# The scan stage of a hybrid linear-attention layer: squares of finished rows put behind the copies of the largest level, attention heads taken by PSUM bank, state and output products of one direction together

## The chip, the core and the metric

The kernel runs on one core of a Trainium2 chip. The time is the device time of one execution in microseconds. TensorE (PE) has two clock levels in the profile, 1.2 and 2.4 GHz; the column "PEclk" of a view gives the granted clock as a share of the higher one.

## What is computed

One layer over 2048 latent tokens (16 chunks of 128 rows here) after a prefix of 256 context tokens (two chunks). Two bidirectional linear-attention mixers run on the same normalized input: GLA (a gate for each key dimension, 4 heads of 64 keys and 128 values) and Gated DeltaNet (delta rule, 4 heads of 128). Each latent scan starts from the last context state of its direction. In the scan stage, per chunk and direction:

```
# GLA
att = einsum('bhtd,bhsd,bhtsd->bhts', q, k, exp(b_t - b_s))      # causal, decay for each key dimension
o   = einsum('bhtd,bhde->bhte', q * exp(b), s) + att @ v
s   = s * exp(b_last) + einsum('bhsd,bhse->bhde', k * exp(b_last - b), v)
# Gated DeltaNet
v_new = u - w @ s
o     = (q * exp(g)) @ s + aqk @ v_new
s     = s * exp(g_last) + (k * exp(g_last - g))^T @ v_new
# both: the two directions are added, then
y = rmsnorm(o_f + rev(o_b), onorm) * silu(gate)
```

After the scan stage both y go through their output weights, are merged by gates and projected; a residual and a last RMSNorm follow.

## The kernel before, in words

The program runs in three stretches: projections and preparation (to about 1366 us), the scan stage (`phase_mix`, 1366 to 1812), the output products (from 1812, where PE is full again). The change lies in the scan stage alone.

The scan stage has a context step and 16 latent steps. Step `si` takes one chunk from the front (direction 0, "f") and one from the back (direction 1, "b"). In step s the GLA attention of the new pair is built (`gla_step`), and the outputs of the pair loaded a step earlier are made: GDN by `gdn_scan`, one generator for each direction, GLA by `gla_state` and `gla_out`. From the middle on every chunk has been met by both directions, so each step finishes four rows of heads: two of GDN (tile `oi`) and two of GLA (tile `og`). `finish` then takes the squares of the finished row (four instructions on ACT, L1409, with an accumulator read each), a logarithm and an exponential as root (L1410, L1411, ACT), the product (L1412, POOL), four transposes (L1416, PE) and the product with the gate (L1417, DVE); until then (the first half) the outputs go to DRAM.

The order on each engine comes from three things. The generators are woven: `weave` gives each its turn in a fixed proportion, and a `yield` ends a turn. A list scheduler then orders all instructions by program order as priority, by waits, and by the slots of the tile pools; an engine runs its instructions in the order that results. Last, `behind` ties one instruction after another in that order, without a semaphore.

The pieces that the change and the prediction speak of:

- `gdn_scan`: L1055 (w @ s), L1066 (q @ s), L1077 (v_new, read by DVE L1079 into `vn`), then the state product L1087 (read by DVE L1091 into `Sb`) and the output product L1097 (read by DVE L1098 into `oi`). Each is 4 matmuls in the program, 8 in the trace, for a direction. All put their result into a PSUM tile `pz`, of which there are three in rotation.
- `gla_group`: decay sums (L1125, PE, from the gate g that ACT L132 splits into halves after its load), exponentials (L1213, L1216, ACT), products with q (L1222, DVE, `ql`) and k (L1223, POOL, `E`).
- `gla_lev`: level products (L1264, PE), in two groups a step: 32 instructions in the program for levels 64, 32, 16, 8 (64 in the trace), then 16 for levels 4 and 2. The level 64 is copied by ACT (L1272) into `at`, the others by DVE into `own` (L1275). The second group waits for its PSUM slots to be read.
- `gla_ones` and `gla_near`: level 1; DVE L1238 and POOL L1239 make `qk`, PE L1246 multiplies it, ACT L1236 its exponential, L1252 copies `own` into `at`.
- `gla_out`: the products of attention and v (L1346) go into two PSUM tiles, heads 0 and 2 into the first, 1 and 3 into the second; L1354 adds the products with the state; ACT (L1362) or DVE (L1364) reads them into `og`.

```
        for h in range(4):
            nc.tensor.matmul(po[h % 2][:, 0, h // 2], f["at"][:, h], f["v"][:, h * P:(h + 1) * P],
                             start=h < 2, stop=False, skip_group_check=True)
```

Of the kernel before, what the change touches and what calls it, by code (L numbers as in the profile page):

```python
# [16 lines left out]
AF = mybir.ActivationFunctionType  # L17
# [80 lines left out]
class Build:  # L98
# [945 lines left out]
    def gdn_scan(self, r, need_o, end=False):  # L1044
        nc, wk = self.nc, self.wk
        d, c = r["d"], r["c"]
        S = self.Sb[d]
        B4 = [P, 4, P]
        col = lambda t, h: t[:, c, 4 * d + h:4 * d + h + 1]
        if S is None:  # L1050
            rhs = r["v"]
        else:
            ps = self.heads(self.pv())
            for h in range(4):
                nc.tensor.matmul(ps[:, h], r["kT"][:, h, :], S[:, h], start=True, stop=True)  # L1055
            rhs = wk.tile(B4, F32, name="rhs")
            for h in range(4):
                nc.vector.scalar_tensor_tensor(rhs[:, h], ps[:, h], col(self.negeg, h), r["v"][:, h],
                                               op0=ALU.mult, op1=ALU.add)
            yield  # L1060
        if need_o:
            l = c - NCTX
            prev = r["prev"]
            po = self.heads(self.pv())
            for h in range(4):
                mm = nc.tensor.matmul(po[:, h], r["qT"][:, h, :], S[:, h], start=True, stop=True)  # L1066
            self.fin_rest(2, mm)
            oi = prev if prev is not None else self.op.tile(B4, F32, name="oi", bufs=4)
            for h in range(4):
                if prev is None:  # L1070
                    nc.scalar.mul(oi[:, h], po[:, h], col(self.eg, h))
                else:
                    nc.vector.scalar_tensor_tensor(oi[:, h], po[:, h], col(self.eg, h), prev[:, h], op0=ALU.mult, op1=ALU.add)
            yield
        ps = self.heads(self.pv())
        for h in range(4):
            nc.tensor.matmul(ps[:, h], r["ub"][:, h], rhs[:, h], start=True, stop=True)  # L1077
        vn = wk.tile(B4, F32, name="vn")
        nc.vector.tensor_tensor(vn, ps, self.bc(self.beta, c, d), op=ALU.mult)  # L1079
        yield  # L1080
        if not end:
            S2 = self.st.tile(B4, F32, name=f"Sb{d}")
            if S is not None:
                nc.gpsimd.tensor_tensor(S2, S, self.bc(self.egl, c, d), op=ALU.mult)
            ps = self.heads(self.pv())
            for h in range(4):
                nc.tensor.matmul(ps[:, h], r["kt"][:, h], vn[:, h], start=True, stop=True)  # L1087
            if S is None:
                nc.vector.tensor_copy(S2, ps)
            else:  # L1090
                nc.vector.tensor_tensor(S2, S2, ps, op=ALU.add)  # L1091
            self.Sb[d] = S2
            yield
        if need_o:
            po = self.heads(self.pv())
            for h in range(4):
                nc.tensor.matmul(po[:, h], r["at"][:, h], vn[:, h], start=True, stop=True)  # L1097
            nc.vector.tensor_tensor(oi, po, oi, op=ALU.add)  # L1098
            yield
            yield from self.put_o(1, l, oi)  # L1100
# [153 lines left out]
    def gla_lev(self, levs, behind=None):  # L1254
        nc, got = self.nc, []
        for r, ks, ql, m in levs:
            ps = self.slot()
            for ct in range(2):
                for x in range(2):
                    y = x if m < 64 else 1 - x  # L1260
                    keys, qs = slice(64 * x, 64 * x + 64), slice(64 * y, 64 * y + 64)
                    for hp in range(2):
                        rows = slice(64 * hp, 64 * hp + 64)
                        mm = nc.tensor.matmul(ps[keys, hp, ct], ks[ct][rows, keys], ql[rows, ct, qs], start=True, stop=True)  # L1264
                        self.behind(mm, behind)
                        self.last_lev = mm
            got.append((r, ps, m))
        for r, ps, m in got:
            if m == 64:
                for x in range(2):  # L1270
                    rows, cols = slice(64 * x, 64 * x + 64), slice(64 - 64 * x, 128 - 64 * x)
                    nc.scalar.copy(self.byhalf(r["at"])[rows, :, :, cols], ps[rows])  # L1272
            else:
                i = LEVELS.index(m) - 1
                nc.vector.copy_predicated(self.byhalf(r["own"]),  # L1275
                                          self.am[:, i].unsqueeze(1).unsqueeze(1).broadcast_to([P, 2, 2, 64]), ps)
# [64 lines left out]
    def gla_out(self, pair, S):  # L1341
        nc = self.nc
        f = pair[0]
        po = [self.pv().rearrange("p (d c t) -> p d c t", d=2, c=2) for _ in range(2)]
        for h in range(4):
            nc.tensor.matmul(po[h % 2][:, 0, h // 2], f["at"][:, h], f["v"][:, h * P:(h + 1) * P],  # L1346
                             start=h < 2, stop=False, skip_group_check=True)
        for d, r in enumerate(pair):
            for ct in range(2):
                for x in range(2):  # L1350
                    half = slice(64 * x, 64 * x + 64)
                    for hp in range(2):
                        rows = slice(64 * hp, 64 * hp + 64)
                        mm = nc.tensor.matmul(po[hp][half, d, ct], r["qe"][rows, ct, half], S[d][rows, ct], start=False,  # L1354
                                              stop=d == 1 and ct == 1, skip_group_check=True)

        def done():
            o = self.og = f["prev"] if f["prev"] is not None else self.op.tile([P, 2, 4, P], F32, name="og")
            v = lambda t, hp: t.rearrange("p d (c h) t -> p h d c t", h=2)[:, hp]
            for hp in range(2):  # L1360
                if f["prev"] is None:
                    nc.scalar.copy(v(o, hp), po[hp])  # L1362
                else:
                    nc.vector.tensor_tensor(v(o, hp), v(f["prev"], hp), po[hp], op=ALU.add)  # L1364
        return mm, done
# [34 lines left out]
    def finish(self, mi, l, src):  # L1400
        nc, wk = self.nc, self.wk
        if "o" in self.dbg:
            nc.sync.dma_start(self.dbg["o"][mi, l], self.flat(src))
        y = wk.tile([P, 4, P], F32, name="fg", bufs=4)
        nc.sync.dma_start(y, self.d_gb[l, :, 4 * mi:4 * mi + 4, :])
        sq = wk.tile([P, P], BF16, name="fsq", bufs=1)
        ss = wk.tile([P, 4], F32, name="fss", bufs=4)
        for h in range(4):
            nc.scalar.activation(sq, src[:, h], AF.Square, accum_out=ss[:, h:h + 1])  # L1409
        nc.scalar.activation(ss, ss, AF.Ln, bias=self.eps, scale=1.0 / 128)  # L1410
        nc.scalar.activation(ss, ss, AF.Exp, scale=-0.5)  # L1411
        nc.gpsimd.tensor_tensor(src, src, ss.unsqueeze(2).broadcast_to([P, 4, P]), op=ALU.mult)  # L1412
        mm = yield
        pt = self.pe()
        for h in range(4):
            self.behind(nc.tensor.transpose(pt[:, h * P:(h + 1) * P], src[:, h], self.ident), mm)  # L1416
        nc.vector.scalar_tensor_tensor(self.flat(y), pt, self.pc[:, 64 + mi:65 + mi], self.flat(y),  # L1417
                                       op0=ALU.mult, op1=ALU.mult)
        nc.sync.dma_start(self.d_y[l, :, mi * 4:mi * 4 + 4, :], y)
        yield  # L1420
# [18 lines left out]
    def phase_mix(self):  # L1439
        nc = self.nc  # L1440
# [26 lines left out]
        self.gq = self.pool("gq", 2, ctx=gctx)  # L1467
        self.ppe = self.pool("ppe", 3, PSUM, ctx=ctx)
        self.lv = self.pool("ppg", 1, PSUM, ctx=gctx).tile([P, 2, 4, 2, 64], F32, name="lv")
        self.nslot, self.last_lev = 0, None  # L1470
        self.seen, self.fin = [{}, {}], []
        self.Sa, self.Sb = [None, None], [None, None]
        order = [(2 + s, NCH - 1 - s) for s in range(NLAT)]
# [425 lines left out]
```

## Time and profile before

| | |
|---|---|
| median of 3 runs | 2144.94 us (2143.9 to 2147.0) |
| profiled execution | 2138.93 us, span of its instructions 2136.9 us |
| mean granted clock | 0.987 |
| busy, share of the span | PE 96%, DVE 60%, ACT 43%, POOL 38% |
| scan stage, 1366 to 1812 us | PE 393.2 of 446 us busy, granted clock 0.96 |
| before it and after it | PE 1334.6 of 1366 us and 314.1 of 324.9 us, clock 1.00 and 0.99 |

A step of the scan is measured from one first L1264 to the next; these begin at 1385.66 (first latent step), 1415.85, 1439.38, 1464.12, 1486.05, 1510.13, 1531.99, 1554.13, 1578.21, 1599.78, 1625.91, 1653.97, 1679.61, 1706.00, 1734.43 and 1761.10 us. Finished rows begin with the step from 1599.78.

How to read the views: a group of equal instructions is written as engine, line, operation, output<-inputs, shapes, count. "[0.38 <-DVE oi L1098]" is the time in which the engine stood still before the group, and the instruction whose end released it. Busy times of the stretches are sums within the stretch; DMA share is that of the core's 16 DMA engines.

### The profile page before, as it was taken

How to read it: one execution, taken by the hardware profiler on the slowest of the kernel's cores; microseconds unless marked ns; L12 is line 12 of the kernel's file. 1: busy time of each engine (PE TensorE's matmuls, PEld its weight loads, DVE VectorE, ACT ScalarE, POOL GpSimd, SP SyncE). 2: the span in 40 equal slices, each digit the busy share in tenths (PEclk: the TensorE clock that was granted, in tenths of full speed). 3: DMA queues.
4: the chain of work that ended last, by engine and by line, in shares of the span. 5: the costliest groups of instructions: out<-in, count | busy, mean ns of one | idle time of the engine just before them, and what ended most of it. 6: DMA issues, size and time to landing. Idle time of an engine off the chain costs nothing.

```text
span 2136.9 us, 40356 instructions
## 1 busy us (share of the span) xinstructions
PE 2041.9 (96%) x15208; PEld 1674.4 (78%) x15208; DVE 1283.2 (60%) x2229; ACT 914.5 (43%) x2208; POOL 816.7 (38%) x746
## 2 busy tenths in 40 slices
PE   6999999999999999999999999899988888999998
PEld 2688888888888888777777777688888876787786
DVE  2713555556667653555555655466567776576776
ACT  3645245555543223444344444345545656002332
POOL 2410122222221104566666665256556656002211
PEclk9999999999999999999999999999999999999999
DMA  8323122222222224443344443688888877898543
GB/s 285 111 86 119 48 58 76 63 62 65 73 63 72 72 72 133 149 143 129 122 146 141 159 144 110 202 306 284 296 291 297 296 250 233 286 317 300 181 147 111
DMA packets 272862, 346.96 MB, mean 162 GB/s; under 512 B 25000, under 2 KB 176796, under 8 KB 272668
## 3 DMA queue, kind: packets, MB, share of 16 engines
q1 hardware_dynamic: 272668, 344.39, 48.8%
q8 instruction: 120, 1.97, 0.4%
q14 instruction: 74, 0.61, 0.1%
HBM read 218.73 MB, written 125.57 MB: 161 GB/s over the span
## 4 chain that ended last, share of the span: by engine, by line
PE 72%; DMA 7%; issue 7%; DVE 6%; ACT 5%; POOL 3%; SPq 1%; DVEq 0%; POOLq 0%; ACTq 0%
PE pz L371 46%; PE pm L1605 3%; PE pz L1605 2%; DMA g<-dg 2%; PE pe L943 1%; PE pe L1125 1%; PE pl L1002 1%; PE pl L995 1%; PE pz L1087 1%; DMA ga<-dgate 1%; PE pl L1003 1%; DVE ql L1222 1%; ACT E L1216 1%; PE pp L1823 1%; PE pz L1066 1%
## 5 line engine op out<-in xcount | busy, mean ns | idle before, releaser
L371 PE MATMUL pz<-hi,wh 128*128 128x512 f32 (+1 forms) x1560 | 621.2, 399 | 1.1 <-DVE hi L134 1.1
L371 PE MATMUL pz<-lo,wh 128*128 128x512 f32 (+1 forms) x1560 | 600.1, 385 | 1.8 <-POOL lo L135 1.8
L371 PE MATMUL pz<-hi,wl 128*128 128x512 f32 (+1 forms) x1520 | 588.1, 387 | 0.0
L371 PEld LDWEIGHTS pz<-lo,wh 128*128 128x128 f32 x1560 | 294.6, 189 | 51.2 <-POOL lo L135 3.7
L371 PEld LDWEIGHTS pz<-hi,wh 128*128 128x128 f32 x1560 | 294.1, 189 | 47.1 <-DVE hi L134 1.7
L371 PEld LDWEIGHTS pz<-hi,wl 128*128 128x128 f32 x1520 | 285.9, 188 | 53.7 <-issue 0.4
L135 POOL TENSOR_TENSOR wl<-w,wh 128x1024 fp32r<-128x1024 f32 x44 | 109.6, 2491 | 437.5 <-ACT wh L132 314.2
L575 DVE SCALAR_TENSOR_TENSOR acc<-zpad,cw,acc 128x1024 f32<-128x1024 f32 x192 | 269.5, 1403 | 6.6
L880 DVE CAST_PREDICATED U<-kit,pl 128x256 f16<-128x256 int32 x216 | 91.3, 432 | 138.7 <-PE pl L1003 135.0
L996 ACT CAST ppb<-pl 128x256 f16<-128x256 f32 x216 | 73.8, 374 | 169.9 <-PE pl L995 163.2
L1605 PE MATMUL pm<-y,wb 128*128 128x512 f32 x480 | 118.5, 399 | 5.2 <-DVE ga L1608 2.9
L1223 POOL TENSOR_TENSOR E<-E,ak 128x256 f32<-128x256 f32 x96 | 79.4, 847 | 111.5 <-ACT E L1216 67.0
L135 DVE TENSOR_TENSOR sql<-sq,sqh 128x512 fp32r<-128x512 f32 (+1 forms) x36 | 28.0, 804 | 142.7 <-ACT sqh L132 142.5
L1605 PEld LDWEIGHTS pm<-y,wb 128*128 128x128 f32 x480 | 90.9, 191 | 26.9 <-DVE y L135 2.6
L630 POOL TENSOR_TENSOR acc<-acc,sq 128x512 f32<-128x512 f32 x32 | 50.6, 1590 | 138.7 <-ACT sq L629 90.9
L560 ACT COPY zpad<-pz 128x512 f32<-128x512 f32 x48 | 28.2, 588 | 137.5 <-PE pz L371 137.5
L1125 PE MATMUL pe<-wt,gh 128*128 128x256 f32 x264 | 77.0, 320 | 8.8 <-ACT E L1216 4.9
L880 DVE CAST_PREDICATED Tm<-kit,pl 128x256 f16<-128x256 int32 x180 | 76.4, 425 | 0.0
L1002 PEld LDWEIGHTS <-Tm 128*128 128x128 f16 x864 | 55.1, 98 | 26.5 <-issue 22.0
L132 ACT CAST wh<-w 128x1024 fp32r<-128x1024 f32 x44 | 46.2, 1049 | 68.6 <-PE pz L371 56.0
L1216 ACT ACTIVATE E<-pe 128x128 f32<-128x128 f32 x320 | 64.5, 306 | 18.7 <-PE pe L1125 18.1
L1222 DVE TENSOR_TENSOR ql<-E,q 128x256 f32<-128x256 f32 x96 | 64.1, 694 | 13.6 <-ACT E L1213 11.7
(326 smaller groups left out, 4265.3 us busy)
## 6 DMA issues: line engine op xcount, KB each, us to landing
gd<-dgd SPq DMA_DIRECT2D x32, 768.0 KB, 7.8
w<-in_w_in SPq DMA_DIRECT2D x44, 512.0 KB, 3.5
dgate<-ob SPq DMA_DIRECT2D x128, 128.0 KB, 1.8
qk<-dqkv SPq DMA_DIRECT2D x32, 512.0 KB, 5.9
ga<-dgate SPq DMA_DIRECT2D x64, 256.0 KB, 4.7
x<-in_x SPq DMA_DIRECT2D x28, 512.0 KB, 5.0
dqkv<-acc SPq DMA_DIRECT2D x192, 64.0 KB, 1.6
dgd<-tm SPq DMA_DIRECT2D x36, 256.0 KB, 2.5
```

What stands on the lines that cost most here:

```text
L135: getattr(nc, lo).tensor_tensor(dst_lo, src, dst_hi.bitcast(F32), op=ALU.subtract)
L371: nc.tensor.matmul(ps[:, 0:n], a[:, kk, :], b[:, kk, :], start=(k == 0), stop=(k == last - 1))
L575: nc.vector.scalar_tensor_tensor(acc, src, wcol, acc, op0=ALU.mult, op1=ALU.add)
L630: nc.gpsimd.tensor_tensor(v, v, r, op=ALU.mult)
L880: self.nc.vector.copy_predicated(out, mv, data)
L996: nc.scalar.copy(ppl, pc.rearrange("p h (j i) -> p h j i", i=m))
L1002: nc.tensor.matmul(pu[:, h], Tm[:, h], ppl[:, h], start=True, stop=True)
L1125: self.nc.tensor.matmul(out, g[:, i, ct * P:(ct + 1) * P], self.wt[:, d, cols[0]:cols[1]], start=(j == 0), stop=(j == 1))
L1216: nc.scalar.activation(E[:, ct, li, x].rearrange("p (j e i) -> p e j i", e=2, i=m), s[:, x * P:(x + 1) * P].rearrange("p (e j i) -> p e j ...
L1222: nc.vector.tensor_tensor(ql[:, li], E[:, :, li, 0], q, op=ALU.mult)
L1223: nc.gpsimd.tensor_tensor(E[:, :, li, 1], E[:, :, li, 1], k, op=ALU.mult)
L1605: nc.tensor.matmul(ps, self.wab[j // 2][wi][:, 4 * i + k, (j % 2) * P:(j % 2) * P + P], yy[:, k, :], start=(n == 0), stop=(n == 11))
```

## The change

No instruction is added or removed. A `yield` between the state and the output product of a direction goes, so the two are issued in one turn; `gla_out` takes the heads in the order 0, 2, 1, 3; the ACT copies of level 64 are remembered as `self.far`, and the squares in `finish` are tied behind the last of them.

```diff
@@ gdn_scan
                 nc.vector.tensor_tensor(S2, S2, ps, op=ALU.add)
             self.Sb[d] = S2
-            yield
         if need_o:
@@ gla_lev
-                    nc.scalar.copy(self.byhalf(r["at"])[rows, :, :, cols], ps[rows])
+                    self.far = nc.scalar.copy(self.byhalf(r["at"])[rows, :, :, cols], ps[rows])
@@ gla_out
-        for h in range(4):
+        for h in (0, 2, 1, 3):
@@ finish
-            nc.scalar.activation(sq, src[:, h], AF.Square, accum_out=ss[:, h:h + 1])
+            self.behind(nc.scalar.activation(sq, src[:, h], AF.Square, accum_out=ss[:, h:h + 1]), self.far)
@@ phase_mix
-        self.nslot, self.last_lev = 0, None
+        self.nslot, self.last_lev, self.far = 0, None, None
```

Below, lines after 1093 are one lower in the changed kernel (L1097 is L1096 there, L1272 is L1271, L1409 is L1408). PE at the end of a first-half step, before (`vn`, `gd`, `av` are the inputs named above; gh and gl the halves of the gate):

```order
L1087 MATMUL pz<-vn,gd 128x128 x8
L1125 MATMUL pe<-wt,gh_16745 128x2x128
L1125 MATMUL pe<-wt,gl_16746 128x2x128
L1125 MATMUL pe<-wt,gh_16745 128x2x2x64
L1125 MATMUL pe<-wt,gl_16746 128x2x2x64
L1143 MATMUL pe<-kf,E_16776 128x128 x2
L1097 MATMUL pz<-vn,gd 128x128 x8
L1346 MATMUL pz<-av,at 128x128 x4
L1354 MATMUL pz<-Sa_16461,q_16381 64x128 x8
```

and the same place in the changed kernel:

```order
L1087 MATMUL pz<-vn,gd 128x128 x4
L1096 MATMUL pz<-vn,gd 128x128 x4
L1087 MATMUL pz<-vn,gd 128x128 x4
L1096 MATMUL pz<-vn,gd 128x128 x4
L1124 MATMUL pe<-wt,gh_16745 128x2x128
L1124 MATMUL pe<-wt,gl_16746 128x2x128
L1124 MATMUL pe<-wt,gh_16745 128x2x2x64
L1124 MATMUL pe<-wt,gl_16746 128x2x2x64
L1142 MATMUL pe<-kf,E_16776 128x128 x2
L1345 MATMUL pz<-av,at 128x128 x4
L1353 MATMUL pz<-Sa_16461,q_16381 64x128 x8
```

The output product of direction 0 moved ahead of the state product of direction 1, and four L1125 moved behind both outputs. DVE at the same place, before:

```order
L1079 TENSOR_TENSOR vn<-pz,beta 128x512
L1091 TENSOR_TENSOR Sb_17224<-Sb_17224,pz 128x512
L1091 TENSOR_TENSOR Sb_17232<-Sb_17232,pz 128x512
L1222 TENSOR_TENSOR ql<-E,q_17061 128x256 x2
L1098 TENSOR_TENSOR oi<-pz,oi 128x512 x2
```

and changed:

```order
L1079 TENSOR_TENSOR vn<-pz,beta 128x512
L1091 TENSOR_TENSOR Sb_17224<-Sb_17224,pz 128x512
L1097 TENSOR_TENSOR oi<-pz,oi 128x512
L1091 TENSOR_TENSOR Sb_17238<-Sb_17238,pz 128x512
L1097 TENSOR_TENSOR oi<-pz,oi 128x512
L1221 TENSOR_TENSOR ql<-E,q_17061 128x256 x2
```

Each `oi` moved right behind its `Sb`, ahead of the two `ql`. ACT in a second-half step, from the copies of level 64 on, before:

```order
L1409 ACTIVATE fsq,fss<-og 128x128 x4
L1272 COPY at<-lv 64x2x2x64 x2
L1216 ACTIVATE E<-pe 128x2x16x4 x2
L1216 ACTIVATE E<-pe 128x2x32x2 x2
L1145 COPY akt<-pe 128x256
L1236 ACTIVATE E_18799<-pe 128x128 x2
L1410 ACTIVATE fss<-fss,cb 128x4
L1409 ACTIVATE fsq,fss<-oi 128x128
L1411 ACTIVATE fss<-fss 128x4
L1409 ACTIVATE fsq,fss<-oi 128x128 x3
```

and changed:

```order
L1271 COPY at<-lv 64x2x2x64 x2
L1215 ACTIVATE E<-pe 128x2x16x4 x2
L1215 ACTIVATE E<-pe 128x2x32x2 x2
L1144 COPY akt<-pe 128x256
L1235 ACTIVATE E_18799<-pe 128x128 x2
L1408 ACTIVATE fsq,fss<-oi 128x128 x4
L1409 ACTIVATE fss<-fss,cb 128x4
L1408 ACTIVATE fsq,fss<-oi 128x128
L1410 ACTIVATE fss<-fss 128x4
L1408 ACTIVATE fsq,fss<-oi 128x128 x2
```

The four squares of the first og moved from ahead of the copies to behind all squares of oi. The products of `finish` follow on POOL (og's L1412 behind those of oi) and PE (L1416: oi, oi, og, og in place of og, oi, oi, og, with all eight matmuls of L1077 ahead of the last).

## Rows read from the trace of the kernel before

**Rows 1.** The page: busy time, share of the span and number of matmuls of PE; the chain that ended last, share of the span by engine.

```profile
PE 2041.9 (96%) x15208; PEld 1674.4 (78%) x15208; DVE 1283.2 (60%) x2229; ACT 914.5 (43%) x2208; POOL 816.7 (38%) x746
...
PE 72%; DMA 7%; issue 7%; DVE 6%; ACT 5%; POOL 3%; SPq 1%; DVEq 0%; POOLq 0%; ACTq 0%
```

**Rows 2.** The table by stretch. Columns: from:to us, length, then busy us (and instructions) of PE, PE's weight loads, DVE, ACT, POOL, then granted clock, DMA share, GB/s. The stretches are eight steps, six steps, and two single steps.

```profile
1415.85:1599.78 183.93, 167.92 (x2280) 153.64 (x2276) 118.61 (x267) 97.93 (x364) 107.25 (x130) 0.99 0.82 289
1599.78:1761.10 161.32, 140.92 (x1766) 131.10 (x1762) 121.07 (x276) 94.75 (x458) 101.05 (x116) 0.95 0.84 285
1415.85:1439.38 23.53, 22.51 (x317) 19.63 (x313) 14.69 (x33) 12.28 (x46) 13.47 (x16) 1.00 0.86 319
1653.97:1679.61 25.64, 22.13 (x299) 20.31 (x295) 20.05 (x46) 15.77 (x76) 17.36 (x20) 1.00 0.90 295
```

**Rows 3.** What PE waited for from 1368 to 1600 us (the first half and the context step). Columns: us in total, times, longest.

```profile
PE pz L1346 <- DVE oi L1098: 5.9, 8, 1.9
PE pz L1087 <- DVE vn L1079: 5.0, 9, 1.3
PE lv L1264 <- POOL E L1223: 3.4, 10, 0.4
```

**Rows 4.** The timeline of PE in the first half: one step's end, and two L1087 of which the first direction waits. Columns: start, length in us, engine, line, operation, and the wait before it.

```profile
1408.87 2.05 PE L1087 MATMUL pz<-vn,gd 128*128 128x128 f32 x16 [0.61 <-DVE vn L1079]
...
1456.70 1.05 PE L1087 MATMUL pz<-vn,gd 128*128 128x128 f32 x8
1458.08 1.16 PE L1087 MATMUL pz<-vn,gd 128*128 128x128 f32 x8 [0.33 <-DVE vn L1079]
...
1459.78 1.95 PE L1097 MATMUL pz<-vn,gd 128*128 128x128 f32 x16
1461.56 0.39 PE L1346 MATMUL pz<-av,at 128*128 128x128 f32 x2
1462.33 0.94 PE L1346 MATMUL pz<-av,at 128*128 128x128 f32 x6 [0.38 <-DVE oi L1098]
...
1593.98 2.05 PE L1087 MATMUL pz<-vn,gd 128*128 128x128 f32 x16 [1.34 <-DVE vn L1079]
```

**Rows 5.** The timeline of all engines around PE's longest wait of the first half, columns as in rows 4.

```profile
1502.91 1.17 ACT L132 CAST gh<-g 128x512 fp32r<-128x512 f32 x2 [2.07 <-DMA g<-dg]
...
1504.29 2.05 DVE L1222 TENSOR_TENSOR ql<-E,q 128x256 f32<-128x256 f32 x2 [1.10 <-ACT E L1216]
...
1506.99 1.45 PE L1346 MATMUL pz<-av,at 128*128 128x128 f32 x6 [1.90 <-DVE oi L1098]
```

**Rows 6.** The table by stretch, columns as in rows 2: three stretches of low granted clock.

```profile
1507.40:1510.90 3.50, 3.50 (x74) 3.28 (x76) 0.14 (x1) 0.49 (x2) 1.88 (x3) 0.53 0.49 181
1722.40:1725.70 3.30, 3.30 (x17) 3.30 (x16) 1.79 (x5) 0.72 (x3) 0.15 (x1) 0.50 0.68 224
1633.80:1640.20 6.40, 6.40 (x37) 6.05 (x38) 3.93 (x13) 4.57 (x22) 4.99 (x6) 0.50 0.62 182
```

**Rows 7.** What PE waited for from 1600 to 1812 us (the second half), columns as in rows 3.

```profile
PE lv L1264 <- DVE own L1275: 6.8, 6, 1.5
PE pe L1246 <- POOL qk L1239: 6.1, 6, 1.5
PE pe L1416 <- POOL og L1412: 6.0, 4, 2.5
```

**Rows 8.** The timeline of all engines in the step from 1706.00 us, columns as in rows 4.

```profile
1706.00 1.11 PE L1264 MATMUL lv<-ql,E 64*64 64x64 f32 x64
...
1706.96 0.31 ACT L1409 ACTIVATE fsq<-og 128x128 bf16<-128x128 f32 x1 [5.86 <-DVE og L1364]
...
1708.05 0.31 ACT L1409 ACTIVATE fsq<-og 128x128 bf16<-128x128 f32 x1
...
1708.48 0.31 ACT L1409 ACTIVATE fsq<-og 128x128 bf16<-128x128 f32 x1
...
1708.79 0.73 ACT L1272 COPY at<-lv 64x256 f32<-64x256 f32 x2
...
1710.44 0.51 ACT L1236 ACTIVATE E<-pe 128x128 f32<-128x128 f32 x2
...
1711.69 0.69 PE L1264 MATMUL lv<-ql,E 64*64 64x64 f32 x32 [0.79 <-DVE own L1275]
1711.73 1.08 POOL L1412 TENSOR_TENSOR og<-og,fss 128x512 f32<-128x512 f32 x1
...
1713.82 0.61 PE L1246 MATMUL pe<-bones,qk 128*128 128x2 f32 x4 [1.01 <-POOL qk L1239]
...
1717.09 0.40 ACT L1252 COPY at<-own 64x256 f32<-64x256 f32 x1
...
1718.90 0.62 ACT L132 CAST gh<-g 128x512 fp32r<-128x512 f32 x1 [1.08 <-DMA g<-dg]
...
1721.92 0.81 PE L1416 MATMUL pe<-kf,og 128*128 128x128 f32 x4 [2.28 <-POOL og L1412]
...
1730.73 1.95 PE L1097 MATMUL pz<-vn,gd 128*128 128x128 f32 x16
1732.52 1.06 PE L1346 MATMUL pz<-av,at 128*128 128x128 f32 x8
1733.50 1.10 PE L1354 MATMUL pz<-Sa,q 64*64 64x128 f32 x32
```

## The prediction

> **What bounds the kernel now.** I read the page first [rows 1]: TensorE (PE) is busy for 2041.9 us, 96% of the span, and the chain that ended last runs through it for 72%, so only what stops PE, or lowers its clock, can move the time. Then the table by stretch [rows 2]: the scan stage is where PE is not full. Its first eight latent steps after the first (from 1415.85 us; no row is finished yet) take 183.93 us with 167.92 busy, 23.0 us a step; the six from 1599.78 (rows are finished, their squares run on ACT) take 161.32 with 140.92 busy, 26.9 a step. Granted clock 0.99 and 0.95: the second part loses clock as well as time. Then PE's waits in each half [rows 3, 7], and the timelines of single steps for what stands ahead of each wait [rows 4, 5, 8]. The reader is to see that the first half's waits are short, on DVE, and at two places, and the second half's sit behind one long ACT queue.
>
> **First half: state and output products of one direction together.** No instruction is added or removed; all of the change is order. Now PE runs L1087 for both directions, then L1097 for both, then L1346. Two waits follow from this.
>
> (a) The second direction's L1087 waits for its vn, which DVE makes last: 0.33 us in the step shown [rows 4]. Of the 5.0 us in 9 such waits [rows 3] two are the first direction's (0.61 and 1.34, [rows 4]) and stay, since nothing is put ahead of them. The other seven are 3.05 us. In the new order the first direction's L1097 (eight matmuls; the sixteen of both directions take 1.78) stands between: 0.9 us of cover against waits of 0.3 to 0.6. I take all 3.05 as removed.
>
> (b) L1346 stops after two of its matmuls, for a PSUM buffer that DVE frees by oi L1098: 5.9 us, 8 times, longest 1.9 [rows 3], 0.38 in the step shown [rows 4]. DVE does Sb, Sb, two ql, and only then the two oi. The buffers rotate by three, so L1346's second buffer is the one that held the first direction's output. In the new order this output starts right behind the first direction's L1087, at 1457.6 instead of 1459.78 in the step shown, its oi runs right behind its Sb, ahead of the ql, and the buffers asked for are those of the first oi and the second Sb. I take 5.9 as removed. The head order (0, 2, 1, 3) moves the use of the second buffer two matmuls later, 0.22 us; once the wait is gone that is worth nothing. What changing buffers at every matmul costs by itself is bounded by eight L1346 in 0.98 us against 0.90 for eight L1097 [rows 8]: at most 0.1 a step, 1.5 over all steps; I take 0, since L1346 also ends in matmuls of another shape.
>
> (c) The longest of these, 1.90 us, was ACT's cast waiting 2.07 us for the DMA of g, then ql, then oi [rows 5]. Behind it the clock stood at 0.53 for 3.5 us [rows 6]: the lower level, 1.2 GHz, after PE had stood still. At half speed 3.5 us do the work of 1.86, so 1.64 us go with it.
>
> What it may cost: the four L1125 that stood between L1087 and L1097 now come behind both outputs, so exp (ACT), ql (DVE) and E (POOL) for the next L1264 start later. From the step shown I place the last E 0.3 us ahead of its use: bounds 0 and, from L1264's wait on E that is there already (3.4 us in 10, [rows 3]), another 0.4 a step, 3.2 in all. I take 1.0, nearer the end where it is hidden. Sum of the first half: -3.05 - 5.9 - 1.64 + 1.0 = **-9.6 us**.
>
> **Loads.** The first half moves 289 GB/s x 183.93 us = 53.2 MB; at the most a step of the trace shows, 319 GB/s [rows 2], that is 167 us. The shortened half needs about 175 (one of the eight L1346 waits lies ahead of it), so transfers allow it, with 5% to spare. The Trainium skill (Perfetto Trace Analysis, Roofline) puts the ceiling of one core's 16 DMA engines at about 435 GB/s; by that the estimate is 122 us, and no step here comes near that rate. Both leave the sum as it is; the thin margin of the measured rate is the reason for a rival.
>
> **Second half: squares behind the copies.** Now ACT holds four squares of og ahead of the at copies. They wait for DVE's og (5.86 us idle before the first) and run one every 0.43 us, so the copies start 2.8 us into the step [rows 8]. DVE's own waits for the copies, PE's second L1264 for own (0.79), and POOL, with og's L1412 (1.08) ahead of qk's L1239, holds PE's L1246 (1.01) [rows 8]. In all: own 6.8 us, qk 6.1, and L1416 on og 6.0 [rows 7], 18.9 us over the six steps and the last one, 2.7 a step.
>
> After: the copies start when the first L1264 ends, at about +1.1 us; L1236 ends near +3.9 where it now ends at 1710.95, +4.95. The waits on own and qk (12.9 us) go. But all sixteen squares stand behind L1236 now, not twelve. From L1236's end to the last square now takes 6.5 us (to 1717.49, the end of the L1252 behind it [rows 8]); four squares more are 1.74, a cast of gh and the roots about 0.9, and the cast waits for its DMA, 1.08 in this step: the last og is normalized by L1412 (1.08) and reaches PE at 3.9 + 6.5 + 1.74 + 0.9 + 1.08 + 1.08 = +15.2 us; without the DMA wait +14.1. PE came to its last og L1416 at 1719.64, +13.6, with 0.79 and 1.01 of waits that go and with four L1077 (0.9) that now come before it: +12.7. So PE waits 1.4 to 2.5 us at its two og transposes, where 2.7 a step go now. The work behind them is the same. Bounds: 1.3 a step gained, or, with twice the DMA wait, 3.6 waited and 0.9 lost; I take **0**, by the row with the DMA wait in it. That POOL now runs og's L1412 behind those of oi costs nothing more: it is made when ACT's root comes.
>
> Clock: 0.95 over 161.32 us is 16 us at 1.2 GHz, 8 us lost. The 2.28 us wait was followed by 0.50 over 3.3 us [rows 6, 8]; the step at 1653.97, with four short waits, kept 1.00 [rows 2]. The new waits are few and long, so I leave the 8 us as it is. The Trainium skill (TensorE: Matmul & The Clock Gate, A second HAM failure mode) says the reverse: frequent micro-idles between groups of matmuls make the clock fall and rise. By that, merging four waits into two would give clock back; the trace bears it out less than the other reading, and what it would give is the third rival.
>
> The context step ahead and the last step are reordered too; I see nothing on the path there: 0, bounds +-2 us.
>
> **Sum**: -9.6 + 0 + 0 = -9.6 us on a profiled execution of 2138.93. That one is 6.0 us under the median of the runs, 2144.94; against the median the forecast is 2135.3. About 0.2% (4.3 us) is what a measurement can tell from no change.
>
> **Rivals.**
> 1. *The squares' tail decides (slower).* Every second-half step waits 3.6 us at og, and the clock falls behind it for 6.4 us, as it did once [rows 6]: 3.2 us lost a step. Over 6.5 steps (the last counted half): 6.5 x 0.9 + 6.5 x 3.2 - 8 = +18.7, less 9.6: 2154. It decides from +2.1 us a step. For: the ACT chain is longer than PE's way to the transposes. Against: the chain starts 1.05 us earlier.
> 2. *The first half gives it back.* The g loads are late already (2.07, [rows 5]); what PE gains it loses at E or ql. Half of 9.6 stays, and the second half costs 2: 2142.
> 3. *The clock comes back.* PE's waits in the second half merge and the 8 us go: 2127.5. For: 2.7 us of waits at three places become 1.4 at one. Against: the 2.28 us wait of [rows 8].
> 4. *The order does not change as said*, so nothing happens. The printed order of PE, ACT and DVE excludes that; I give it no chance.
>
> **Chances.** Forecast 0.54 (2131 to 2140, by the bounds 0 to 3.2 and +-2); rival 3 0.18; rival 2 0.18; rival 1 0.10. Faster 0.72, same 0.18, slower 0.10. The range goes from a little beyond rival 3, 2126, to between rivals 2 and 1, 2146.
>
> **What would show it.** In the changed profile: L1346 without a wait on oi, and the second L1087 without one on vn; eight first-half steps in about 175 us at clock 1.00; L1264's wait on E below 0.8. In the second half: no wait on own, a shorter one on qk, L1416 on og at 10 to 18 us in all, steps near 26.9, copies at +1.1 and the last square near +12 to +14. The forecast is wrong if L1264 waits over 1 us on E or ql in the first half, if second-half steps differ from 26.9 by over 1 us, or if stages outside the scan move.

## The result, and the profile after

| | before | changed |
|---|---|---|
| first comparison, median | 2144.42 us (6 runs) | 2126.41 us (2123.3 to 2130.07, 6 runs) |
| ratio, 95% interval | | 0.9922 [0.9904, 0.9941] |
| second comparison | 2140.76 us (17 runs) | 2128.32 us (6 runs), 0.9934 [0.9919, 0.9949] |
| profiled executions | 2138.93, span 2136.9 | 2126.90, span 2125.1 |

The change is faster by 0.7 to 0.8%; 2135.3 us with a range of 2126.0 to 2146.0 had been forecast, so the first median lies 0.4 us inside the range. The two profiled executions differ by 12.0 us, the first medians by 18.0. The table by stretch of the changed kernel (columns as in rows 2; eight first-half steps, six finishing steps, and a piece of the first finishing step), from one L1353 to the next, answers to [rows 2]:

```profile
1416.37:1589.27 172.90, 165.02 (x2274) 151.81 (x2273) 121.51 (x268) 97.23 (x363) 107.16 (x130) 1.00 0.86 302
1589.27:1748.35 159.08, 138.37 (x1753) 128.66 (x1752) 122.34 (x276) 95.00 (x455) 102.86 (x117) 0.96 0.87 296
1603.00:1611.00 8.00, 5.44 (x28) 5.44 (x29) 2.65 (x7) 5.42 (x28) 5.16 (x6) 0.57 0.71 224
```

The first half goes from 183.93 to 172.90 us at clock 1.00, the six finishing steps (those from which finished rows are made) from 161.32 to 159.08 at clock 0.96. The context step ends 1.4 us later, and what follows the six steps takes 376.8 us for 376.7. PE's waits in the first half (us in total, times, longest; [rows 3] before):

```profile
PE lv L1263 <- POOL E L1222: 5.5, 14, 0.8
...
PE pz L1087 <- DVE vn L1079: 1.2, 2, 0.7
```

L1346 (now L1345) waits no more, and of the waits on vn the two of the first direction are left. The wait on E has grown, from 3.4 us in 10. The same place as in [rows 4], PE's timeline in the changed kernel:

```profile
1456.05 1.05 PE L1087 MATMUL pz<-vn,gd 128*128 128x128 f32 x8
1456.94 1.06 PE L1096 MATMUL pz<-vn,gd 128*128 128x128 f32 x8
1458.03 1.16 PE L1087 MATMUL pz<-vn,gd 128*128 128x128 f32 x8
1459.02 1.06 PE L1096 MATMUL pz<-vn,gd 128*128 128x128 f32 x8
...
1460.61 1.06 PE L1345 MATMUL pz<-av,at 128*128 128x128 f32 x8
1461.60 1.10 PE L1353 MATMUL pz<-Sa,q 64*64 64x128 f32 x32
1462.52 1.11 PE L1263 MATMUL lv<-ql,E 64*64 64x64 f32 x64
```

The four products of the two directions run one behind the other, and L1345 runs its eight matmuls in one piece: no group has a wait in brackets. PE's waits in the second half ([rows 7] before):

```profile
PE pe L1415 <- POOL oi L1411: 10.6, 3, 4.4
PE pe L1415 <- POOL og L1411: 7.7, 6, 2.4
PE lv L1263 <- POOL E L1222: 3.9, 11, 0.6
...
PE pe L1245 <- POOL qk L1238: 0.8, 1, 0.8
```

None is on own any more and 0.8 us is left on qk, but 18.3 us are at the transposes (L1415), 10.6 of them on oi, in three waits. The timeline of all engines in the first finishing step shows what stands ahead of one of these:

```profile
1591.37 0.75 ACT L1271 COPY at<-lv 64x256 f32<-64x256 f32 x2 [0.43 <-PE lv L1263]
...
1593.68 0.56 ACT L1235 ACTIVATE E<-pe 128x128 f32<-128x128 f32 x2
...
1596.44 0.31 ACT L1408 ACTIVATE fsq<-oi 128x128 bf16<-128x128 f32 x1
...
1601.88 0.62 ACT L132 CAST gh<-g 128x512 fp32r<-128x512 f32 x1 [5.03 <-DMA g<-dg]
...
1602.40 0.30 ACT L1408 ACTIVATE fsq<-oi 128x128 bf16<-128x128 f32 x1
...
1604.47 1.03 POOL L1411 TENSOR_TENSOR oi<-oi,fss 128x512 f32<-128x512 f32 x1
...
1605.56 1.12 PE L1415 MATMUL pe<-kf,oi 128*128 128x128 f32 x4 [4.39 <-POOL oi L1411]
```

The copies start 1.2 us after the L1263 at 1590.19, as intended. But between two squares of oi stands the cast gh, which waits 5.03 us for its load. The squares behind it are late, then POOL's product, then PE, which waits 4.39 us, and the granted clock is 0.57 from 1603 to 1611 us (last row of the table above).

### The profile page after: what moved, and what is told of

The parts are those of the page before. It is cut to its first block, busy times and chain, and to the rows that moved or that the text cites. A ratio compares the mean times of both kernels' runs of the same rounds, so it can differ in the third digit from the quotient of the medians.

```text
span 2125.1 us, 40362 instructions
## 1 busy us (share of the span) xinstructions
PE 2037.5 (96%) x15208; PEld 1670.0 (79%) x15208; DVE 1282.5 (60%) x2229; ACT 914.1 (43%) x2208; POOL 818.2 (38%) x746
## 4 chain that ended last, share of the span: by engine, by line
PE 71%; DMA 9%; issue 6%; POOL 5%; DVE 4%; ACT 4%; SPq 1%; DVEq 0%; POOLq 0%; ACTq 0%
PE pz L371 46%; PE pm L1604 3%; DMA g<-dg 2%; PE pz L1604 2%; PE pe L943 1%; PE pl L1002 1%; PE pl L995 1%; PE pl L1003 1%; POOL E L1222 1%; DMA dm<-ga 1%; PE pe L1124 1%; PE pp L1822 1%; PE pq L620 1%; PE pz L1087 1%; PE pz L1077 1%
## 5 line engine op out<-in xcount | busy, mean ns | idle before, releaser
L630 POOL TENSOR_TENSOR acc<-acc,sq 128x512 f32<-128x512 f32 x32 | 51.3, 1611 | 137.8 <-ACT sq L629 89.9
L1124 PE MATMUL pe<-wt,gh 128*128 128x256 f32 x264 | 74.7, 313 | 4.5 <-ACT E L1133 2.7
```

What stands on the lines that cost most here:

```text
L630: nc.gpsimd.tensor_tensor(v, v, r, op=ALU.mult)
L1124: self.nc.tensor.matmul(out, g[:, i, ct * P:(ct + 1) * P], self.wt[:, d, cols[0]:cols[1]], start=(j == 0), stop=(j == 1))
```

## Experiments

Lengths of the six finishing steps, from one L1354 (L1353) to the next, us; the ratio is to the runs of before in the same comparison, on one chip, with its 95% interval. Beside the first comparison there are three, each on its own chip: e0, e1, e2 and e4; e5, e7, e8 and e9; e10, e11, e12 and a0.

```
kernel                          first half  finishing steps 1 to 6                    ratio
before                          183.93      26.12 28.06 25.64 26.40 28.42 26.68
before again (a0_before)        180.66      26.37 26.13 27.56 27.70 28.37 25.12       0.9994 [0.9981, 1.0007]
change                          172.90      29.59 27.46 25.77 26.55 25.91 23.80       0.9922 [0.9904, 0.9941]
change again (e0_change)        174.04      27.66 27.98 26.48 26.14 26.39 23.81       0.9934 [0.9919, 0.9949]
yield alone (e1_yield)          175.27      29.30 28.39 25.39 26.80 26.84 25.22       0.9950 [0.9931, 0.9968]
tie of squares alone (e2_far)   183.58      26.20 29.45 28.59 26.21 27.41 23.80       0.9995 [0.9982, 1.0009]
change, old heads (e5)          174.11      29.43 28.83 27.13 25.87 26.35 23.81       0.9950 [0.9931, 0.9969]
change, cast last (e4)          176.37      23.43 24.30 24.24 24.22 24.23 24.21       0.9866 [0.9848, 0.9884]
  e4, old heads (e10)           176.69      23.42 24.26 24.23 24.25 24.22 24.25       0.9887 [0.9867, 0.9907]
  e4, no tie of squares (e8)    175.19      26.55 28.02 26.27 28.14 29.34 28.41       0.9975 [0.9963, 0.9988]
  e4, cast behind row 3 (e9)    178.08      24.03 24.10 24.06 24.05 24.05 23.93       0.9876 [0.9856, 0.9895]
  e4, three buffers of g (e12)  170.76      23.43 24.25 24.23 24.24 24.22 24.24       0.9856 [0.9834, 0.9878]
cast last alone (e7)            183.37      25.32 25.31 25.29 25.31 25.31 25.31       0.9949 [0.9933, 0.9964]
change, three buffers (e11)     171.86      26.50 23.88 23.88 23.88 31.04 23.81       0.9898 [0.9878, 0.9918]
```

**The parts.** The yield alone:

```diff
             self.Sb[d] = S2
-            yield
```

> The kernel before with one edit alone: no yield between the state and the output product of a direction. Theory A (the first half's gain is this edit's, the second half's is the tie's): the eight first-half steps fall from 183.9 to about 173 us, with no wait of L1346 on oi; in the second half the copies of level 64 stand behind squares still (here eight of oi and four of og in place of four of og), PE waits for own 1 to 2 us a step, and the steps are no shorter than 26.9: -9 to -11 us against before. Theory B (the squares' place matters for the amount of ACT work behind L1236, not for the copies): only four squares stay behind L1236, L1416 waits less than 2 us in all, and the second half gains 4 us or more as well: -14 us or better.

It took 2132.72 us, 0.9950: theory A, though by the medians the gain is 8.0 us where 9 to 11 had been said. The first half has the change's length within 2.4 us (175.27 against 172.90 and 174.04); in the second the waits on the ACT copies' readers are there as before:

```profile
PE pe L1245 <- POOL qk L1238: 6.6, 6, 1.5
PE lv L1263 <- DVE own L1274: 5.6, 6, 1.6
```

Theory B falls: the transposes do not wait here (no such row), but the six steps together are no shorter for it, 161.94 us for 161.32. The squares tied, alone (the edits of `gla_lev`, `finish` and `phase_mix` in the diff above):

> The kernel before with the squares tied behind the copies of level 64 alone. The first half is as before (183.9 us for eight steps). Theory A: waits on own and qk (12.9 us) go and come back at the transposes (10 to 18 us on oi and og): second half 0 +-3 us, total 0 +-3. Theory B (the tie is what gains): -5 us or better. Theory C (the ACT chain that is longer behind L1236 decides): +3 us or worse.

2140.34 us, 0.9995, no difference: theory A, wait for wait. The waits on own are gone, those on qk are 0.8 us, and the transposes have taken them over:

```profile
PE pe L1416 <- POOL oi L1412: 15.9, 6, 4.6
PE pe L1416 <- POOL og L1412: 3.3, 2, 2.6
...
PE pe L1246 <- POOL qk L1239: 0.8, 1, 0.8
```

The change itself once more:

> The change once more, beside its parts: ratio 0.990 to 0.994, -12 to -20 us. If the profile taken here is 12 us under a typical profile of before, the 18 us between the medians came from a low profile of before, not from a stage that the two profiles do not show. First half near 173 us, second half near 187 us from the first finishing step on.

2128.32 us. The steps show the same picture in a second profile.

**Is it the cast?** The change, with the cast tied behind the last square:

```diff
-            nc.scalar.copy(dst_hi, src)
+            self.behind(nc.scalar.copy(dst_hi, src), after)
...
-        self.split(*r["gg"], r["g"])
+        self.split(*r["gg"], r["g"], after=self.lastsq)
...
-            self.behind(nc.scalar.activation(sq, src[:, h], AF.Square, accum_out=ss[:, h:h + 1]), self.far)
+            self.lastsq = nc.scalar.activation(sq, src[:, h], AF.Square, accum_out=ss[:, h:h + 1])
+            self.behind(self.lastsq, self.far)
```

> The change, with ACT's cast of the gate (gh, which waits for the DMA of g) also tied behind the last square, so that squares no longer stand behind a late load. Theory A (in the changed kernel the transposes wait because squares stand behind this cast: 10.6 us on oi in 3 times, 7.7 us on og in 6): the waits on oi fall below 2 us, those on og stay near 8, and it is 4 to 9 us faster than the change. Rival (loads set the pace, the wait moves to the next user of g): L1125 or L1264 waits on ACT or POOL by as much, within 3 us of the change.

2114.29 us, 0.9866: 14 us faster than the change on the same chip, more than the 4 to 9 of theory A. The six finishing steps (columns as in rows 2) and the end of one of them:

```profile
1592.72:1737.35 144.63, 134.44 (x1753) 123.52 (x1752) 119.48 (x276) 97.92 (x456) 100.26 (x116) 1.00 0.89 315
```

```profile
1653.45 0.60 ACT L132 CAST gh<-g 128x512 fp32r<-128x512 f32 x1
...
1654.10 0.39 PE L1124 MATMUL pe<-wt,gh 128*128 128x256 f32 x1 [0.72 <-ACT gh L132]
...
1654.69 0.53 PE L1416 MATMUL pe<-kf,oi 128*128 128x128 f32 x3
...
1655.91 0.71 PE L1416 MATMUL pe<-kf,oi 128*128 128x128 f32 x5
...
1656.82 1.09 PE L1416 MATMUL pe<-kf,og 128*128 128x128 f32 x8
```

The clock is 1.00, the steps are equal to 0.1 us but for the first, and no transpose waits in them, not on oi and, against theory A, not on og either; L1124 waits for the cast instead, 4.4 us in all. The scheduler also set the sixteen transposes behind the first L1124 that use the cast, so PE comes to them when all squares are done. So the cast's place and the transposes' place moved together here; e11 below takes the cast's wait away and leaves the transposes where they were. The six steps fell by 14.45 us: PE's listed waits in them add up to 9.1 us where they were 19.9 in the change, and PE's busy time fell from 138.37 to 134.44 with the clock.

The cast moved alone, in the kernel before:

> The kernel before, with only the cast of the gate (gh) tied behind the last square; squares, yield and heads as before. Theory A (the late gate is a cost of its own): L1416's wait on og, 6.0 us of before, falls by half, the waits on own and qk (12.9 us) stay: -2 to -6 us. Rival (it is the tie of the squares behind the copies that exposes the cast; before has few squares behind it): within 2 us of before.

2130.61 us, 0.9949: nearly twice the upper end of theory A. The steps are 25.31 us, all of them to 0.03, and the clock is 1.00. PE's long wait is one a step, at L1234, ahead of own and qk; the waits on own and qk, which theory A had staying, are gone:

```profile
PE pe L1234 <- ACT E L1216: 8.9, 6, 1.5
```

```profile
1598.65:1750.50 151.85, 135.72 (x1755) 123.93 (x1754) 118.34 (x276) 95.91 (x456) 101.07 (x117) 1.00 0.86 305
```

So the late cast cost the kernel before as well: PE's listed waits in the six steps add up to 16.2 us for 20.0, and its busy time is 135.72 for 140.92, which is the clock. As in e4, the scheduler moved part of PE's order with the cast (all sixteen L1066 now stand ahead of the transposes), and for this kernel no run separates the two.

And the cast last without the tie of the squares:

> One direction's products together, head order, and the cast gh behind the last square, but without the tie of the squares behind the copies. Theory A (the tie pays only once the late cast is out of the squares' way): waits on own and qk come back, 10 to 13 us in the second half, steps of about 26 us instead of 24.2, total -16 to -20 us against before. Rival (the tie is worth its 1 to 4 us as in the change): -24 us or better.

```diff
             self.lastsq = nc.scalar.activation(sq, src[:, h], AF.Square, accum_out=ss[:, h:h + 1])
-            self.behind(self.lastsq, self.far)
```

2136.87 us, 0.9975, slower than both theories said. With the yield gone the eight squares of oi also come ahead of the copies, the waits on own are 9.1 us in five, and the clock is 0.92:

```profile
PE lv L1263 <- DVE own L1274: 9.1, 5, 1.8
```

```profile
1590.22:1756.95 166.73, 148.55 (x1760) 134.96 (x1759) 121.17 (x276) 99.11 (x461) 102.29 (x117) 0.92 0.82 282
```

The tie of the squares, which by itself is worth nothing that the runs can tell (e2, 0.9995), is worth some 23 us here (0.9975 to 0.9866, two comparisons): theory A in kind, low in size, since it left out the clock. Of the 22.1 us between the six steps of e8 and e4, 14.1 are PE's busy time.

One row earlier (the cast behind the third row's squares):

> The change with the cast gh tied behind the third of the four finished rows' squares instead of the last. Theory A (behind the last square the cast comes 0.7 us late a step for L1124, 4.4 us in 6): this wait falls below 1 us and the steps to 23.5 us, -31 us against before. Rival (the load of g is late by more than the squares of one row, so the cast stops the fourth row): waits of 1 to 3 us at the last og transposes, -20 to -27 us.

```diff
-        self.split(*r["gg"], r["g"], after=self.lastsq)
+        self.split(*r["gg"], r["g"], after=self.gate)
...
-            for g in self.fin:
+            for i, g in enumerate(self.fin):
                 next(g)
+                if i == len(self.fin) - 2:
+                    self.gate = self.lastsq
```

2116.16 us, 0.9876, as e4 within the intervals. L1124's wait on the cast goes, as theory A said, and a wait at og takes its place, as the rival said:

```profile
PE pe L1416 <- POOL og L1412: 5.8, 6, 1.0
...
PE pe L1124 <- ACT gh L132: 0.2, 1, 0.2
```

**The heads.** The change with the old order of heads, and e4 with it:

```diff
-        for h in (0, 2, 1, 3):
+        for h in range(4):
```

> The change without its head order (heads 0, 1, 2, 3 in L1346). Theory A (the head order is worth nothing once the wait on oi is gone): as the change, -12 to -16 us against before, no wait of L1345 in the first half. Rival (alternating buffers costs PE, up to 0.1 us a step by the rows of before, or the second buffer is asked for 0.22 us too early): 1 to 4 us slower than the change, L1345 with waits on DVE or longer from its start to L1353's.

2132.55 us, 0.9950, 7 runs from 2124.78 to 2138.29. That leans to the rival, but L1345 has no wait in the first half and takes 9.5 us for the same 72 matmuls from 1400 to 1595 us in both kernels; the longer steps are the second and third finishing ones, with the late cast. The intervals of e5 and the change overlap, so what the heads do beside a late cast stays open.

> The change with the gate's cast behind the last square (its runs spread over 5 us only), but with heads 0, 1, 2, 3. Theory A (the head order is worth nothing; the 3 us between the change and its version without it came from the spread of the late gate's steps): ratio 0.985 to 0.988, within 2 us of the same kernel with heads 0, 2, 1, 3, and no wait of L1345. Rival (alternating buffers cost): 2 to 4 us slower than with heads 0, 2, 1, 3, in steps longer by 0.1 to 0.25 us each.

2116.35 us, 0.9887, beside e4's 0.9866 on another chip: the intervals overlap. The six steps take the same time to the last digit:

```profile
1591.76:1736.39 144.63, 134.43 (x1753) 123.51 (x1753) 119.46 (x276) 97.92 (x456) 100.32 (x116) 1.00 0.89 313
```

The ratio misses theory A's bound by 0.0007, the steps bear it out: with the cast last the head order is worth nothing that a finishing step shows.

**Why is g late?** Three buffers instead of two, in the change and in e4:

```diff
-            r["g"] = wk.tile([P, 2 - d, 256], F32, name=f"g{d}")[:, 0:n]
+            r["g"] = wk.tile([P, 2 - d, 256], F32, name=f"g{d}", bufs=3)[:, 0:n]
```

> The change with three buffers for the gate g instead of two, so that its load is issued earlier; ACT's order of cast and squares nearly as in the change. Theory A (g is late because its load is issued late): ACT's wait for the DMA of g falls from 18.3 us to below 6 in the same stretch, the waits of L1415 on oi from 10.6 to below 3, and it is 5 to 12 us faster than the change. Rival (g is late because all transfers are behind at the change of halves): the wait moves to another load (oi, og, gate rows, qk), within 3 us of the change.

2117.75 us, 0.9898. What ACT waits for from 1570 to 1780 us, in the change and then here (us, times, longest), and PE's transposes here:

```profile
ACT gh L132 <- DMA g<-dg: 18.3, 6, 5.3
```

```profile
ACT gh L132 <- DMA g<-dg: 8.4, 2, 5.4
```

```profile
PE pe L1415 <- POOL og L1411: 11.2, 11, 6.2
PE pe L1415 <- POOL oi L1411: 4.1, 5, 1.9
```

Theory A holds for most: 18.3 us fell to 8.4, four of the six steps take 23.9 us, and by the ratios it is 5 to 8 us faster than the change. One late load of 5.4 us is left, and makes one step 31.04; the transposes wait 4.1 us on oi, where less than 3 was expected, and 11.2 on og, 6.2 of it in that step. Since only the number of buffers differs, most of the loads had been late because they were issued late.

This run also separates what moved together in e4. In its second to fourth finishing steps ACT waits for no load of g. The cast still stands between squares of oi (somewhat earlier among them), and the transposes still stand ahead of the L1124 that use the cast, as in the change. The three steps in one row, and parts of the third (columns as in rows 2 and rows 4):

```profile
1612.53:1684.17 71.64, 67.17 (x878) 61.95 (x877) 62.19 (x140) 46.98 (x228) 51.95 (x61) 1.00 0.91 315
```

```profile
1641.90 0.69 ACT L132 CAST gh<-g 128x512 fp32r<-128x512 f32 x1
...
1646.97 0.60 PE L1415 MATMUL pe<-kf,oi 128*128 128x128 f32 x4
...
1648.45 0.66 PE L1415 MATMUL pe<-kf,oi 128*128 128x128 f32 x4 [0.43 <-POOL oi L1411]
```

They take 23.88 us each at clock 1.00, less than e4's 24.2. So it was the cast's wait for its load that made these steps of the change long, not the place of the transposes, and a cast that does not wait may stand among the squares.

> Both: the cast behind the last square and three buffers for g. Theory A (with the cast behind the squares the load's time no longer matters): within 2 us of the kernel with the cast moved alone, ratio 0.984 to 0.988. Rival (the first finishing steps still lose to late loads): 2 to 5 us faster than it.

2109.46 us (2104.71 to 2116.89), 0.9856, the fastest of all; e4's interval overlaps it, so by the ratio it is theory A. Of the profiles, e12's is its fastest execution and e4's its slowest; they show a gain of 5.6 us in the first half, where the last step before the finishing ones falls from 24.35 to 20.12. First e12's two stretches, then what e4 has in that step and e12 has not, a wait for vn and a clock of 0.50 behind it:

```profile
1412.01:1582.77 170.76, 163.25 (x2273) 151.52 (x2273) 118.61 (x268) 97.41 (x362) 108.25 (x130) 1.00 0.88 307
1582.77:1727.38 144.61, 134.39 (x1754) 123.47 (x1753) 119.57 (x276) 97.88 (x456) 100.38 (x117) 1.00 0.90 317
```

```profile
1586.21 1.84 PE L1087 MATMUL pz<-vn,gd 128*128 128x128 f32 x8 [2.44 <-DVE vn L1079]
```

```profile
1586.50:1589.90 3.40, 3.40 (x18) 3.40 (x18) 1.71 (x5) 0.00 (x0) 0.97 (x1) 0.50 1.02 349
```

In the change that step takes 21.45 us; of the kernels with the cast tied and two buffers, e4, e9 and e10 have the longer step, e7 and e8 have not, and no run shows why.

**The kernel before, again:**

> The kernel before itself, for its spread and a second profile: ratio 1.000 +-0.002. If the runs of before differ by 10 us and the profile shown above is a low one, this profile has the same steps in the first half and other lengths (1 to 3 us) in the finishing steps, through late loads or stretches of low clock, and nothing outside the scan.

2138.74 us, 12 runs from 2131.42 to 2143.72, 0.9994. Its stretches, columns as in rows 2, and ACT's wait for g from 1570 to 1780 us:

```profile
1415.04:1595.70 180.66, 166.32 (x2274) 152.13 (x2273) 118.65 (x267) 97.08 (x362) 107.35 (x129) 1.00 0.84 294
1595.70:1756.95 161.25, 140.59 (x1759) 130.92 (x1758) 121.07 (x276) 95.83 (x459) 101.32 (x116) 0.95 0.85 288
```

```profile
ACT gh L132 <- DMA g<-dg: 9.3, 6, 4.8
```

The finishing steps take the same sum in another distribution. The first half is 3.3 us shorter than in the first profile, against what was expected: the step with the 1.90 us wait takes 21.87 for 23.24, and the two behind it are 1.6 us shorter together. With these, 70 runs of before have a median of 2140.8 us, and the 12 of the change 2128.0.

## Why the prediction was right, and where its sizes were off

- *State and output together, (a) and (b)*: right. The wait on oi is gone from L1345, that on vn is down to the two of the first direction, 5.0 to 1.2 us. The yield alone gives the first half (e1), the heads nothing that a finishing step of e10 shows, as priced. Between the two first profiles the waits of (a) and (b) fell by 9.7 us, the wait on E grew by 2.1 and PE's busy time fell by 2.9: together 10.5 of the 11.0 us.
- *(c), the 1.90 us wait and the low clock behind it*: an event of that execution, not of the kernel, as far as two profiles tell. The second profile of before has neither (PE's longest wait in these steps is 1.2 us, the clock is 1.00), and its first half is 180.66. So these 1.64 us of the sum came right by the choice of the profile, not by the mechanism. Against the two profiles of before the eight steps gained 6.6 to 11.0 us; 9.0 of the 9.6 had been put there, about the middle of these.
- *Cost at E*: L1264's wait on E went from 3.4 us in 10 to 5.5 in 14; 1.0 forecast, 2.1 found. Its longest is 0.8, where below 0.8 had been named; in the second profile of the change it is 1.05, just past the 1 us that was to count against the forecast, and in e1, which has the same yield edit, 2.13, in a step of 23.68 us.
- *Loads*: 302 GB/s over the shortened half against some 304 worked out, clock 1.00: they allowed it. The margin was wider than worked out: one step of the changed kernel (1482.05 to 1502.33 us) moves 337 GB/s, above the 319 that was taken as the most. The Trainium skill (Perfetto Trace Analysis, Roofline) names about 435 GB/s as the ceiling of a core's 16 DMA engines, and I wrote that no step here comes near. That is so by steps; in pieces of 0.75 us from 1575 to 1605 us the changed kernel's trace does, and two of them, 440 and 448, lie above that figure (a piece counts the packets that start in it):

```profile
GB/s 404 280 171 138 281 101 273 350 265 270 289 341 333 311 396 388 382 402 287 412 391 404 440 429 423 369 385 410 448 380 412 392 321 338 306 272 346 296 229 314
```

- *Second half 0*: right in size, 161.32 to 159.08 us (158.46 in the second profile), though not by the way described. PE's listed waits in these six steps add up to 20.0 us before and 19.9 now. The step that failed inside it is the cast's place and its wait: I put 1.08 us ahead of the last og, and it was up to 5.03 us in the middle of oi. The last squares end 12.3 to 17.9 us behind the step's first L1263, where +12 to +14 had been forecast; without the cast's wait of each step (5.03, 2.66, 1.62, 2.54, 1.18 and none) that is 12.3 to 13.6. The waits on own and qk went and came back at the transposes, 18.3 us in all where 10 to 18 had been forecast, but on oi more than on og. e2 shows this exchange by itself, 0.9995. The steps have a mean of 26.5 us, near the 26.9 that was named, but three of the six single ones are more than 1 us from it (29.59, 25.77, 23.80).
- *Clock left as it is*: 0.95 to 0.96, right; rival 3 needed it to come back. It came in e4 (1.00), where no listed wait is longer than 0.8 us, and in e7, where none is longer than 1.5. The Trainium skill (TensorE: Matmul & The Clock Gate, A second HAM failure mode) blames frequent micro-idles. Here e7 with one wait of 1.5 us in each step kept 1.00, the change's 4.39 us wait had 0.57 around it and behind it, and e8, with 1.8 us on own in five steps, 0.92. The number of waits does not explain these; their length, or where they stand in a step, may, and no run varied that alone.
- *The anchor*: the sum was -9.6 us on 2138.93, which is 2129.3; it was then set against the median of three runs, 2144.94. Over all runs before is 2140.8 and the change 2128.0, so of the 8.9 us between forecast and first median 4.1 were the three runs of before and 1.6 the first six of the change. The other 3.2, -12.8 against -9.6, are not settled: the pairs of profiles give -7.9 to -13.3. The measured 2126.41 is below the 2131 to 2140 that the forecast's own bounds gave and beside rival 3's 2127.5, but rival 3's clock did not come back: that the number fell there is chance.

Rival 1 (the tail decides) was near in the first three finishing steps, of which two are 0.1 and 3.5 us longer than in the first profile of before and one 0.6 shorter; but the last two are 2.5 and 2.9 shorter. Rival 2's doubt was right about g and mostly wrong about where: the time was lost at the squares; at E it was 2.1 us.

## What to carry to other kernels

When work is moved behind something in an engine's queue, read what else stands in that queue with a wait of its own: here a cast that waits for a load stood between the squares, and tying it behind them was worth 14 us on top of the change, while the tie of the squares alone was worth nothing that could be told and, with the cast out of the way, some 23. Try two such orders together before dropping one. Ask first why the wait is there: a third buffer, which lets the load start earlier, took 5 to 8 us off the change without a tie of the cast. And set a sum that is made against one profile beside that profile, not beside a median of three.

## What the runs showed that I had not expected

- Equal steps: in e4 the finishing steps behind the first agree to 0.1 us (24.21 to 24.30), in e7 all six to 0.03 (25.29 to 25.32), at clock 1.00; in the kernels with the late cast among the squares they differ by 3 to 6 us. The late cast is not the only cause: e8 has it last too, and its steps run from 26.27 to 29.34 at clock 0.92. The runs still spread, 2111.28 to 2116.59 in the four of e4 and 2104.71 to 2116.89 in the five of e12; those of before go from 2131.42 to 2150.08 in 70.
- The clock's price: from the change to e4 PE's busy time in the six steps falls by 3.9 us, for the same 1753 matmuls, at a clock of 1.00 for 0.96; from e8 to e4 by 14.1 us, at 1.00 for 0.92 (1760 and 1753 matmuls).
